# Squares of two groups brought into one step of a state-space scan

## The chip, the cores and the metric

The kernel runs on one core of one Trainium2 chip. The metric is the time of one execution on the device in microseconds (us). A core has engines that run side by side, each with an in-order queue of its own: TensorE (PE in the profile, with PEld for its weight loads), VectorE (DVE), ScalarE (ACT), GpSimd (POOL) and SyncE (SP). An instruction that has to wait holds back all that stand behind it on its engine. Loads are issued from SP's queue and most stores from ACT's; both travel on the same 16 DMA engines. In the profile the DMA queue q1 is the one that SP feeds, and q10 the one that ACT feeds.

## The reference, cut to what matters

One decoder layer: a gated spatial mixer and a Mamba-2 state-space mixer beside each other, merged by gates. The change touches the state-space mixer alone, and in it what comes after the scan:

```python
y_b = ssd_scan(xh, dt, a, bm, cm)                 # 8 groups of 4 heads of 64, chunks of 128 positions
y_b = y_b + xh * d_skip[:, None]
yz = (y_b.reshape(b, s, SSM_D_INNER) * jax.nn.silu(ssm_z)).reshape(b, s, SSM_GROUPS, SSM_D_INNER // SSM_GROUPS)
y_b = rms_norm(yz, ssm_norm_w.reshape(SSM_GROUPS, -1)).reshape(b, s, SSM_D_INNER)
```

The `rms_norm` needs, for each of 8 groups and each of 1024 positions, the sum of the squares of 256 channels. These squares and their sums are what the change moves.

## The kernel before, in words

The program has three long stages: the input projections (up to about 905 us), the state-space stage (to about 1125 us) and the output projections (to the end). All matrix products are split into a high and a low part, so that PE does three products for one.

**The state-space stage.** The scan runs in 32 steps. A step is one group and one pair of chunks (256 positions, called s = 0 to 3). The list `order` (line 1333) takes the groups in pairs: group 0 with s = 0, group 1 with s = 0, group 0 with s = 1, and so on, so even and odd groups alternate. I number the steps by their place n in that list, 0 to 31. In the main loop (lines 1582 to 1592) step n does, in this order: `front` (the products yi within a chunk, and the chunk's state sp), `ahead_of` (work for later steps), `draw` (4 to 6 pairs of matmuls pma of another projection, which fill PE), `back` (the product yn with the incoming state, its evacuation), and `prep` of step n + 2.

**What each engine does for a step.**
- PE: yi, sp, pma, yn, then the products and transposes pc and px for step n + 2.
- ACT: eight exponentials dcy of step n + 2 (line 1167, called decays), two exponentials ea of step n + 3 (line 1155), and the copy bn of step n + 2 (line 1190).
- POOL: a masking select on dcy of step n + 3 (line 1159), which must follow that step's ea; then for the step just done y (1264) and yz (1265); then the products st of the states (1228).
- DVE: the product dcy with pc (1183), xd and xe (1186), the sums into the state st (1236), y (1216) and ym (1262).

Most of them are chained in the order of the program by `link` (line 1111).

**From yz to the norm.** Two steps of a group (s = 0 and 1, or s = 2 and 3) fill one tile yz of two strips of 512 positions. Call that a half, q = 0 or 1. Behind the second of these steps `post` (line 1267) stores both strips to DRAM (`yb_d<-yz`, two DMAs of 256 KB on ACT's queue) and puts down `squares`. `squares` (line 1287) has ACT square both strips in place, so it can start only when the store has read them. Three slots later `sum` (1292) lets POOL add the two strips. Two slots after that `post2` (1296) is put among the `posts`, and the next `front` gives PE four small products pq with 32 output columns each, which sum over the partitions; DVE then writes a row, and ACT stores it (`ms_d`). For q = 1 `post3`, `root` and `post4` follow with a load, a power on POOL (line 1320) and a store. The last pair's q = 1 goes another way (`late_squares`).

**What sets the order.** `later(delay, f)` puts a task down for the slot `slot + delay`, and `run_tasks` counts one slot up and runs what is due. `item` runs it after every front, back and prep, so a step has three slots. `sum` and `root` go to the list `work`, from which `beside_step` takes the first one that is due; `ahead_of` calls it (line 1569). Ranks within an engine are settled by a scheduler at build time; matmuls are pinned in the order of the program.

Of the kernel before, what the change touches and what calls it, by code (L numbers as in the profile page):

```python
# [35 lines left out]
def hybrid_kernel(  # L36
# [56 lines left out]
    def store(dst, src):  # L93
        nc.scalar.dma_start(dst, src)
# [446 lines left out]
    def later(delay, f, *a):  # L541
        tasks.append((slot[0] + delay, f, a))
# [577 lines left out]
    def beside_step():  # L1120

        for w in work:
            if w[0] <= slot[0]:
                work.remove(w)
                w[1](*w[2:])
                return


    class Group:
# [137 lines left out]
        def post(self, q):  # L1267

            g = self.g
            for j in range(2):  # L1270
                store(yb_d[2 * g + j][:, q * 512 : (q + 1) * 512], self.yz[q][:, j])
            yz = self.yz[q]
            if g < NG - 2 or q == 0:
                later(8, self.squares, q, [yz[:, j] for j in range(2)])
            else:
                later(3, self.late_squares)

# [64 lines left out]
    def masks(n):  # L1342
        while done_m[0] < min(n, len(order)):
            g, s = order[done_m[0]]
            groups[g].mask(s)
            done_m[0] += 1

    def decays(n):
        while done_d[0] < min(n, len(order)):
            g, s = order[done_d[0]]  # L1350
            groups[g].decay(s)
            done_d[0] += 1
# [210 lines left out]
    def ahead_of(n):  # L1563

        with tc.high_priority():
            decays(n + 3)
            if n + 1 < len(order) and order[n + 1][1]:
                groups[order[n + 1][0]].mul_state(order[n + 1][1], 0)
            for _ in range(1 if n < 29 else 2):
                beside_step()  # L1570
            masks(n + 4)

# [5 lines left out]
    for n in range(2):  # L1578
        step(n, "front")
        ahead_of(n)  # L1580
        draw(10)
    for n in range(len(order)):
        if n > 1:
            step(n, "front")
            ahead_of(n)
            draw(6 if n == 2 else 4 + n % 2)
        step(n, "back")
        if n == 1:
            draw(4)
        if n + 2 < len(order):  # L1590
            step(n + 2, "prep")
        fetch(n + 6)
    while tasks or work or posts:
# [3 lines left out]
        while posts:  # L1597
            p, q, sq = posts.pop(0)
# [474 lines left out]
```

## Time and profile before

| | us |
|---|---|
| median of 3 runs | 1361.64 (1361.04 to 1362.76) |
| the profiled execution, its own time | 1362.27 |
| its span in the trace | 1360.4 |
| state-space stage, in the trace | about 908 to 1125 |

The profiled execution lies 0.63 us above the median, and 1.9 us of it lie around the span. The granted clock of PE was 0.998 of full speed. Rows of a timeline read: start in us, length in us, engine, line, operation, output<-inputs, shapes, how many instructions (x2), and in brackets how long the engine had been idle and what ended that. ACTq and SPq are DMAs that ACT or SP issue. A run of matmuls is shown a little longer than its place, since its last one drains while the next run starts: the distance of two starts is the cost of a run.

### The profile page before, as it was taken

The numbers are of one execution on the slowest core, as the hardware profiler recorded it, in microseconds if no ns is written. First come the engines' busy times: TensorE is split into PE (matmuls) and PEld (weight loads), VectorE is DVE, ScalarE is ACT, GpSimd is POOL, SyncE is SP. The second block draws the span as 40 slices with busy tenths as digits, with TensorE's granted clock in tenths as the row PEclk, the third lists the DMA queues.
The fourth block names the chain that finished last, engine by engine and source line by source line (L and its number), as shares of the span: only waits on it lengthen the run. The fifth ranks groups of instructions, "written<-read, shape, count | busy, mean of one in ns | idle before, by whom it ended". The sixth has DMA issues, their size and how long they took to land.

```text
span 1360.4 us, 20108 instructions
## 1 busy us (share of the span) xinstructions
PE 1347.0 (99%) x6907; PEld 1114.4 (82%) x6907; DVE 1056.1 (78%) x1731; ACT 800.4 (59%) x1446; POOL 196.1 (14%) x193
## 2 busy tenths in 40 slices
PE   8999999999999999999999999999999999999997
PEld 6688888888888888888888888888888888888886
DVE  4776786787777898688887788358888877959976
ACT  5754666666657665466576655486877834233453
POOL 1000000000000000000000000007798981000002
PEclk9999999999999999999999999999999999999999
DMA  9675444333345667777656866489889878888913
GB/s 292 177 248 142 134 124 124 117 119 122 101 132 155 193 184 231 248 216 246 202 192 193 244 204 186 154 289 318 302 297 311 306 256 291 313 261 317 381 45 124
DMA packets 249577, 288.64 MB, mean 212 GB/s; under 512 B 16860, under 2 KB 196484, under 8 KB 249476
## 3 DMA queue, kind: packets, MB, share of 16 engines
q1 hardware_dynamic: 174868, 203.80, 47.0%
q10 hardware_dynamic: 74544, 83.57, 18.0%
q8 instruction: 54, 0.88, 0.3%
q14 instruction: 47, 0.39, 0.1%
q0 software_dynamic: 64, 0.00, 0.0%
HBM read 199.82 MB, written 87.49 MB: 211 GB/s over the span
## 4 chain that ended last, share of the span: by engine, by line
PE 93%; POOL 3%; DMA 1%; issue 1%; ACT 1%; DVE 1%; SPq 0%; POOLq 0%; DVEq 0%; ACTq 0%
PE xcb L585 6%; PE xz L585 6%; PE xuz L585 6%; PE xx L585 6%; PE xg L585 6%; PE pma L82 5%; PE ox L1914 3%; PE yuz L585 3%; PE yx L585 3%; PE ycb L585 3%; PE yp L1722 3%; PE yz L585 3%; PE vx L990 3%; PE yg L585 3%; PE oy L1914 2%; PE x0p L1722 2%
## 5 line engine op out<-in xcount | busy, mean ns | idle before, releaser
L1159 POOL TENSOR_SCALAR_AFFINE_SELECT dcy<-dcy 128x1024 f32<-128x1024 f32 x32 | 35.3, 1103 | 788.7 <-ACT ea L1155 788.7
L1167 ACT ACTIVATE dcy<-dcy,nacs 128x128 f32<-128x128 f32 x256 | 78.3, 389 | 2.9 <-POOL dcy L1159 2.4
L1183 DVE TENSOR_TENSOR dcy<-dcy,pc 128x1024 f32<-128x1024 f32 x32 | 39.0, 1218 | 8.0 <-PE pc L85 5.8
L1265 POOL TENSOR_TENSOR yz<-y,sl 128x512 f32<-128x512 f32 x32 | 44.7, 1396 | 2.5
L82 PE MATMUL pma<-yh,wah 128*128 128x512 f32 x128 | 43.2, 418 | 0.0
L82 PE MATMUL pma<-yh,wal 128*128 128x512 f32 x128 | 42.6, 413 | 0.0
L82 PE MATMUL pma<-yl,wah 128*128 128x512 f32 x128 | 40.2, 395 | 0.0
L1155 ACT ACTIVATE ea<-dcy 64x512 f32<-64x512 f32 x64 | 39.8, 622 | 0.4
L1190 ACT COPY bn<-pc 128x256 f32<-128x256 f32 x32 | 11.9, 371 | 46.4 <-DVE dcy L1183 44.9
L1060 ACT ACTIVATE ac<-ac 128x1024 f32<-128x1024 f32 x32 | 33.9, 1060 | 8.1 <-DVE ac L1058 7.9
L1264 POOL TENSOR_TENSOR y<-y,ym 128x512 f32<-128x512 f32 (+1 forms) x32 | 37.4, 1170 | 1.8 <-DVE ym L1262 1.8
L1058 DVE SCALAR_TENSOR_TENSOR ac<-c2x,cwt,ac 128x1023 f32<-128x1023 f32 (+2 forms) x24 | 30.7, 1278 | 8.8 <-ACT ac L1056 8.7
L1058 DVE SCALAR_TENSOR_TENSOR ac<-c2cb,cwt,ac 128x1023 f32<-128x1023 f32 (+2 forms) x24 | 30.7, 1278 | 8.2 <-ACT ac L1056 8.0
L1929 POOL TENSOR_TENSOR r<-r,fnw 128x512 f32<-128x512 f32 x4 | 6.1, 1534 | 207.3 <-ACT junk L1927 207.3
L82 PE MATMUL yi<-dcy,xd 128*64 128x128 f32 x512 | 35.0, 279 | 0.0
L1262 DVE TENSOR_TENSOR ym<-yn,ea 128x512 f32<-128x512 f32 (+1 forms) x32 | 19.9, 621 | 18.2 <-PE yn L82 18.0
L1653 DVE SCALAR_TENSOR_TENSOR yn<-yn,par,rb 128x512 f32<-128x512 f32 x32 | 26.1, 822 | 9.1 <-DMA yn<-yb_d 9.1
L82 PE MATMUL sp<-xe,bn 128*128 128x256 f32 x112 | 32.7, 409 | 0.0
L82 PEld LDWEIGHTS yn<-sl,st 128*128 128x128 f32 x224 | 29.8, 191 | 2.8 <-POOL st L1228 0.4
L82 PEld LDWEIGHTS yi<-dcy,xd 128*64 128x64 f32 x512 | 27.3, 136 | 5.7 <-issue 3.2
L1058 DVE SCALAR_TENSOR_TENSOR ac<-c1cb,cwt,ac 128x1023 f32<-128x1023 f32 (+2 forms) x24 | 30.6, 1276 | 1.3 <-ACT ac L1056 1.3
L1022 ACT ACTIVATE vm<-vm,vr 128x128 f32<-128x128 f32 x64 | 25.5, 483 | 10.1 <-DMA vm<-v_d 9.6
(2983 smaller groups left out, 4368.4 us busy)
## 6 DMA issues: line engine op xcount, KB each, us to landing
sl<-s_d SPq DMA_DIRECT2D x32, 768.0 KB
s_d<-ac ACTq DMA_DIRECT2D x32, 512.0 KB
wb_d<-wbb ACTq DMA_DIRECT2D x32, 512.0 KB
dcy<-acs_d SPq DMA_DIRECT2D x32, 512.0 KB
av<-in_w_in_dram SPq DMA_DIRECT2D x36, 256.0 KB
aw<-in_ada_w_dram SPq DMA_DIRECT2D x16, 512.0 KB
wbr<-in_w_proj_b_dram SPq DMA_DIRECT2D x32, 256.0 KB
yb_d<-yz ACTq DMA_DIRECT2D x32, 256.0 KB
```

What stands on the lines that cost most here:

```text
L82: pin(PE.matmul(acc, l, r, start=first, stop=last))
L585: pin(PE.matmul(ps, lw[:, k * P : (k + 1) * P], r[k], start=first and n + k == 0, stop=n == 2 and k == 3, skip_group_check=not first))
L990: pin(PE.matmul(ps[pn][j], l[:, j * P : (j + 1) * P], r, start=nm in ("p1", "p5", "p2") and n + units[i][1] == 0, stop=n == 2 and k == 3, ...
L1058: V.scalar_tensor_tensor(ac[:, s:], cc[:, : S - s], conv_wt[:, 3 - s, i : i + 1], ac[:, s:], op0=ALU.mult, op1=ALU.add)
L1155: link("A", lambda: A.activation(ea[hh * HD : (hh + 1) * HD], dcy.rearrange("p (j e) i l -> p e j (i l)", e=2)[hh * HD : (hh + 1) * HD, hh ...
L1159: link("G", lambda: G.affine_select(out=d8, in_=d8, compare_op=ALU.is_ge, fill=-1e30, base=0, pattern=[[0, 2 * HPG], [1, P]], channel_mult ...
L1167: link("A", lambda: A.activation(dcy[:, h, i, :], dcy[:, h, i, :], AF.Exp, bias=sub[:, i, h : h + 1]))
L1183: link("V", lambda: V.tensor_tensor(d3, d3, pc[:, 0:256].unsqueeze(1).to_broadcast([P, HPG, 256]), op=ALU.mult))
L1264: link("G", lambda: G.tensor_add(y1[:, :, t0:], y1[:, :, t0:], m[:, :, t0:]))
L1265: link("G", lambda: G.tensor_mul(yz, y1, sl[:, 4:6]))
L1722: pin(PE.matmul(ps[j], a[:, v, js], r, start=first and n + k == 0, stop=n == 2 and k == KT - 1, skip_group_check=not first))
L1914: pin(PE.matmul(ps, a[:, tsl], b[:, cs], start=first and n + j == 0, stop=n == 2 and j == 3, skip_group_check=not first))
```

## The change

Two numbers. The odd group's squares are put down for 5 slots instead of 8. The odd group's step is one step, or three slots, behind the even one's, so the squares of both groups fall due in the same slot. And every step may take two items from `work` instead of one, so that both sums can go in one step, and with them both groups' pq in one `front`.

```diff
@@ post
-                later(8, self.squares, q, [yz[:, j] for j in range(2)])
+                later(8 - 3 * (g % 2), self.squares, q, [yz[:, j] for j in range(2)])
@@ ahead_of
-            for _ in range(1 if n < 29 else 2):
+            for _ in range(2):
                 beside_step()
```

No instruction is added or removed. It meets seven halves (both halves of the first three pairs, the first of the last pair). In six of them rows move as in the three places below; in the seventh PE had both pq together already.

**ACT, steps 5 and 6 (first pair, q = 0).** yz_0_8448 is group 0's tile, yz_0_8478 is group 1's, dcy_3_8591 is step 7's decays. The semaphores of the stores of group 1's strips are DMAHW2 and DMAHW5. Before:

```order
L1289 ACTIVATE yz_0_8448<-yz_0_8448 128x512 [waits DMAHW1_49]
L1167 ACTIVATE dcy_3_8591<-dcy_3_8591,nacs 128x128 [waits Pool_49]
...
L1155 ACTIVATE ea_0_8672<-dcy_0_8668 64x512 [waits DMAHW0_49]
L1155 ACTIVATE ea_0_8672<-dcy_0_8668 64x512
L1415 CAST wah_1_8947<-wa_1_8433 128x512 [waits PE_49]
L1528 DMA mt_d_84<-tha_0_8435 128x512 [waits DVE_49]
...
L1190 COPY bn_3_8828<-pc_3_8814 128x256 [waits DVE_49]
L1289 ACTIVATE yz_0_8478<-yz_0_8478 128x512 [waits DMAHW2_49]
L1289 ACTIVATE yz_0_8478<-yz_0_8478 128x512 [waits DMAHW5_49]
```

Now, on ACT in the same place:

```order
L1289 ACTIVATE yz_0_8448<-yz_0_8448 128x512 [waits DMAHW1_49]
L1289 ACTIVATE yz_0_8478<-yz_0_8478 128x512 [waits DMAHW2_49]
L1415 CAST wah_1_8954<-wa_1_8433 128x512 [waits PE_49]
L1528 DMA mt_d_84<-tha_0_8435 128x512 [waits DVE_49]
L1289 ACTIVATE yz_0_8478<-yz_0_8478 128x512 [waits DMAHW5_49]
L1167 ACTIVATE dcy_3_8591<-dcy_3_8591,nacs 128x128 [waits Pool_49]
...
L1155 ACTIVATE ea_0_8672<-dcy_0_8668 64x512 [waits DMAHW0_49]
```

Group 1's two squares, with their waits for that group's store, and the cast wah now stand ahead of step 7's decays and step 8's ea; before they stood behind them.

**POOL, steps 6 and 7.** The sums of the two groups, with the selects of steps 8 and 9. Before:

```order
L1159 AFFINE_SELECT dcy_0_8668<-dcy_0_8668 128x1024
L1264 TENSOR_TENSOR y_2_8761<-y_2_8761,ym_2_8809 128x512
L1265 TENSOR_TENSOR yz_2_8808<-y_2_8761,sl_2_8472 128x2x256
L1228 TENSOR_TENSOR st<-st_8261,cd 128x256
L1293 TENSOR_TENSOR yz_0_8448<-yz_0_8448 128x512
L1159 AFFINE_SELECT dcy_0_8742<-dcy_0_8742 128x1024
```

Now, on POOL in the same place:

```order
L1159 AFFINE_SELECT dcy_0_8668<-dcy_0_8668 128x1024
L1264 TENSOR_TENSOR y_2_8763<-y_2_8763,ym_2_8811 128x512
L1265 TENSOR_TENSOR yz_2_8810<-y_2_8763,sl_2_8472 128x2x256
L1228 TENSOR_TENSOR st<-st_8261,cd 128x256
L1293 TENSOR_TENSOR yz_0_8448<-yz_0_8448 128x512
L1293 TENSOR_TENSOR yz_0_8478<-yz_0_8478 128x512
L1159 AFFINE_SELECT dcy_0_8744<-dcy_0_8744 128x1024
```

Group 1's sum has come forward by one step, right behind group 0's; both still stand behind the select of step 8, which follows step 8's ea.

**PE, front of step 7.** pq are the four products of 32 columns of one group. Before:

```order
L82 MATMUL yi_3_8908<-dcy_3_8591,xd_3_8824 64x128 x8
L82 MATMUL pq_0_8917<-yz_0_8448,ones 32x128 x4
L82 MATMUL sp_3_8924<-xe_3_8826,bn_3_8828 128x256
```

Now, on PE in the same place:

```order
L82 MATMUL yi_3_8909<-dcy_3_8591,xd_3_8826 64x128 x8
L82 MATMUL pq_0_8918<-yz_0_8448,ones 32x128 x4
L82 MATMUL pq_0_8925<-yz_0_8478,ones 32x128 x4
L82 MATMUL sp_3_8932<-xe_3_8828,bn_3_8830 128x256
```

The second pq stood in the front of step 8 before. In the second halves the loads of ssq (SP), the powers (POOL, line 1320) and the stores of ms_d and rs_d (ACT) of the odd group come one step earlier too, next to the even group's.

## The prediction

> **What bounds the kernel now.** I read the page's head first, then the busy time of each engine in the state-space stage (908 to 1125 us), the only stage whose rows move.
>
> ```profile
> span 1360.4 us, 20108 instructions
> core 0: us, PE busy (x) PEld busy (x) DVE busy (x) ACT busy (x) POOL busy (x), PEclk, DMA share, GB/s
> 908.00:1125.00 217.00, 216.85 (x1666) 182.32 (x1665) 178.60 (x309) 151.75 (x393) 173.28 (x165) 1.00 0.88 302
> ```
>
> PE has no gap there: 216.85 of 217 us. So the time changes in two ways only: PE's own work gets shorter, or something makes PE wait. POOL (173.28), DVE (178.60) and the DMA engines (0.88) are close enough behind that a delay of a few us on one of them can reach PE. The timeline of PE shows what the pq cost.
>
> ```profile
> 958.24 1.05 PE L82 MATMUL yn<-sl,st 128*128 128x128 f32 x8
> ...
> 960.33 1.09 PE L82 MATMUL yi<-dcy,xd 128*64 128x128 f32 x16
> 961.35 0.42 PE L82 MATMUL pq<-yz,ones 128*32 128x128 f32 x8
> 961.71 0.70 PE L82 MATMUL sp<-xe,bn 128*128 128x256 f32 x2
> ...
> 1111.75 0.64 PE L82 MATMUL pq<-yz,ones 128*32 128x128 f32 x16
> 1112.33 0.74 PE L82 MATMUL pma<-yl,wah 128*128 128x512 f32 x2
> ```
>
> One group's pq takes 961.71 - 961.35 = 0.36 us of PE. At 1111.75 two groups' pq stand together already and take 1112.33 - 1111.75 = 0.58. Together they save 2 x 0.36 - 0.58 = 0.14 us.
>
> **The gain.** Six pairs come together that did not before: 6 x 0.14 = 0.8 us. That is all that PE's own work can give.
>
> **The cost on ACT.** The timeline of ACT around the first place (first pair, q = 0), and the rows of DMA queue q10, which carries ACT's stores, in three short windows: 952.5 to 953, 953 to 954, and 977 to 978.
>
> ```profile
> 945.87 0.46 ACTq L94 DMA_DIRECT2D yb_d<-yz  x1
> ...
> 950.05 1.15 ACT L1289 ACTIVATE yz<-yz 128x512 f32<-128x512 f32 x2
> 951.11 2.15 ACT L1167 ACTIVATE dcy<-dcy,nacs 128x128 f32<-128x128 f32 x7
> ...
> 953.45 0.61 ACT L1155 ACTIVATE ea<-dcy 64x512 f32<-64x512 f32 x1
> 956.30 1.16 ACT L1289 ACTIVATE yz<-yz 128x512 f32<-128x512 f32 x2
> q10 hardware_dynamic: 24, 0.02, 13.9%
> q10 hardware_dynamic: 2, 0.00, 0.6%
> q10 hardware_dynamic: 11, 0.01, 3.9%
> ```
>
> Group 1's second strip is stored from 945.87. Before, its squares came at 956.30, long after. Now they stand behind group 0's, whose two take 951.11 - 950.05 = 1.06: from 951.11. But q10 still moves 0.02 MB between 952.5 and 953, and nearly nothing in the us after; I take the store as done at 953.5, 7.6 us after its issue. So ACT waits there with the decays of step 7 and the ea of step 8 behind it. The first strip's square and the cast wah fit in the wait. The second square ends 953.5 + 0.53 = 954.0, and the decays start then instead of 951.11: **2.9 us late**, of which 1.06 is the squares' own time.
>
> **From ACT to PE.** The rows of POOL, and two of DVE, in the same place:
>
> ```profile
> 954.77 1.09 POOL L1159 TENSOR_SCALAR_AFFINE_SELECT dcy<-dcy 128x1024 f32<-128x1024 f32 x1 [2.04 <-ACT ea L1155]
> 959.47 1.28 POOL L1293 TENSOR_TENSOR yz<-yz 128x512 f32<-128x512 f32 x1
> 961.02 1.09 POOL L1159 TENSOR_SCALAR_AFFINE_SELECT dcy<-dcy 128x1024 f32<-128x1024 f32 x1 [0.27 <-ACT ea L1155]
> 954.78 1.22 DVE L1183 TENSOR_TENSOR dcy<-dcy,pc 128x1024 f32<-128x1024 f32 x1 [0.25 <-ACT ea L1155]
> 957.71 0.41 DVE L1236 TENSOR_TENSOR st<-st,sp 128x256 f32<-128x256 f32 x1
> ```
>
> The select waits for ea (its bracket says so), so it is late by the same 2.9 and starts at 957.7. From its start to group 0's sum POOL is busy without a gap: 959.47 - 954.77 = 4.7. The sum starts at 962.4, and group 1's now follows 1.25 later (1.28 less the overlap of two rows) and ends at 964.9. PE comes to pq at 961.35 and needs both sums: it is held until 964.9, and sp starts 0.36 later. Against before, sp is 965.3 - 961.71 = 3.55 late; the pq that the next step no longer has gives back 0.36. **Net 3.2 us.** On the way PE may already wait at yn for the state st: DVE is late behind the decays (954.78 needs them), st ended at 958.12, and yn's second half needs it at about 958.24 + 0.44. That wait lies inside the one for pq and is not added.
>
> Same steps for the other half of the first pair and for the first half of the second pair; rows of ACT, POOL and PE of each:
>
> ```profile
> 974.03 1.15 ACT L1289 ACTIVATE yz<-yz 128x512 f32<-128x512 f32 x2
> 975.09 2.44 ACT L1167 ACTIVATE dcy<-dcy,nacs 128x128 f32<-128x128 f32 x8
> 983.01 1.28 POOL L1293 TENSOR_TENSOR yz<-yz 128x512 f32<-128x512 f32 x1
> 985.67 1.13 PE L82 MATMUL sp<-xe,bn 128*128 128x256 f32 x4
> ...
> 995.85 1.13 ACTq L94 DMA_DIRECT2D yb_d<-yz  x2
> 998.87 1.16 ACT L1289 ACTIVATE yz<-yz 128x512 f32<-128x512 f32 x2
> 999.93 2.44 ACT L1167 ACTIVATE dcy<-dcy,nacs 128x128 f32<-128x128 f32 x8
> 1008.30 1.28 POOL L1293 TENSOR_TENSOR yz<-yz 128x512 f32<-128x512 f32 x1
> 1010.54 0.70 PE L82 MATMUL sp<-xe,bn 128*128 128x256 f32 x2
> ```
>
> - Second half: q10 ends in 977 to 978 (0.01 MB), done at 978.0. Decays 978.0 + 0.53 instead of 975.09: 3.4 late. Second sum ends 983.01 + 3.4 + 2.53 = 988.9. Net 988.9 - 985.67 = 3.3.
> - Second pair, q = 0: both stores are issued from 995.85. At 7.6 us as in the first place they end near 1003.4; with the cast and one square after that the decays start near 1004.4, 4.5 late. Second sum ends 1008.30 + 4.5 + 2.53 = 1015.3; net 4.8.
>
> The other three I take at the first two's 3.3. Sum: 3.2 + 3.3 + 4.8 + 3 x 3.3 = 21.2 us, the 0.14 being inside (the first pq runs in the wait). Two bounds. **From below**, every store has landed when its square comes: then ACT is late by 1.06 only (1.6 where the cast moves too). First place: 959.47 + 1.6 + 2.53 - 961.71 = 1.9; second: 983.01 + 1.06 + 2.53 - 985.67 = 0.9; third: 1008.30 + 1.6 + 2.53 - 1010.54 = 1.9. Mean 1.6, sum 9.4 us. **From above**, 21.2 and as much as 5 more, if what is late does not catch up (masks behind two powers of POOL in the second halves, banks asked for earlier by the second pq). I take a value nearer to the upper one, 18: the first place goes by rows of a past that the change does not touch, but each stall of 3 us on PE also lets the loads in flight finish before the next ones are issued, so that later stores should land sooner. I take 0.65 off each of the five places behind it.
>
> The powers, loads and small stores that move in the second halves I cost at nothing: they are the same rows one step earlier, behind the longer waits above. If that cover is gone, two powers in one POOL step cost up to the 1.6 us of the second one, three times; this is in the 5 of the upper bound.
>
> The sum is made against the span of 1360.4; the 1.9 us around it stay. Against the median: 1361.64 + 18 = **1379.6 us**.
>
> **Rivals.**
> 1. *The stores are there in time.* The sum is the lower bound: 1361.6 + 9.4 = 1371. For it: the DMA queues get rest in each stall. Against it: in the first place no stall precedes, and q10's rows run past 952.5. By the Trainium skill (DMA: Bandwidth & Descriptors, Anatomy of one DMA) a DMA takes about 2.0 us plus its bytes at 436 GB/s; as an estimate, 512 KB would land some 3.2 us after the issue, ahead of every square, and the time would be this rival's. The trace speaks against that: q10 carries these strips until 952.5 and longer, over 6 us after the issue, since SP's loads are on the same engines (the DMA share is 0.88).
> 2. *Only the switches are saved.* The place is the front of step 7 and its likes: PE stays unheld if the second sum ends before PE gets to the second pq. Then 1361.6 - 0.8 = 1360.8, within what can't be told from no change (0.2% is 2.7 us); with a stall removed elsewhere it could be slightly faster. It decides from the point where POOL gains 1.3 us or so: group 0's sum ends at 960.75, only 0.6 before PE's 961.35, and the second adds 1.25. For it: POOL idled 2.04 us ahead of the select. Against it: that idle ends with ACT's ea, which gets later.
> 3. *The delays feed on themselves.* POOL's lateness makes the next stores, selects and decays late, and no step catches up: 5 us a place, 30 in all, 1392. For it: POOL and DMA are the busiest beside PE. Against it: the step after a pair has two squares and one sum less on ACT and POOL.
>
> **How the numbers follow.** Main case 0.62 (1373 to 1388), rival 1 0.20 (1367 to 1373), rival 2 0.10, split 0.06 no change and 0.04 faster, rival 3 0.08. The range 1367 to 1389 takes the main case and rival 1. Slower by over 0.2%: 0.62 + 0.20 + 0.08 = 0.90.
>
> **What would show it.** Right: the stage grows from 217 us by about 18; ACT waits at line 1289 for `yb_d<-yz`, 1 to 3 us a place; PE's weight loads for pq wait 2 to 3 us for POOL's line 1293, six times; pq rows read x16. Wrong: no such wait of ACT (rival 1 if pq still wait, rival 2 if not); the time lost elsewhere than at pq and yn; or stalls in the step after a pair (rival 3).

## The result, and the profile after

The change makes the kernel slower: median 1395.22 us (1393.06 to 1397.67, 5 runs) beside 1361.75 (1361.04 to 1362.76, 5 runs) of the kernel before, a ratio of 1.0242 with a 95% interval of 1.0231 to 1.0253. That is 33.5 us more; forecast were 18, in a range up to 27 more. The profiled execution took 1397.67 us, the longest of the five; its account below is of its own span.

The page's head and the busy time of the engines by stretch, of the kernel after (columns: stretch, length, then busy us and instructions of PE, PEld, DVE, ACT, POOL, the granted clock of PE, the DMA share, GB/s):

```profile
span 1396.0 us, 20104 instructions
908.00:940.00 32.00, 32.00 (x213) 26.61 (x212) 29.57 (x47) 22.06 (x55) 13.70 (x14) 1.00 0.99 348
940.00:1125.00 185.00, 166.59 (x1278) 139.18 (x1276) 130.52 (x233) 120.57 (x316) 136.11 (x135) 0.96 0.76 256
1125.00:1160.00 35.00, 30.68 (x193) 24.19 (x192) 26.43 (x43) 13.50 (x29) 23.20 (x20) 0.97 0.67 220
1160.00:1396.00 236.00, 229.12 (x1012) 189.74 (x1011) 184.59 (x306) 89.00 (x167) 11.98 (x11) 0.98 0.68 243
```

Two things are new. Between 940 and 1125 PE stands idle for 185 - 166.59 = 18.4 us, where it had no gap before. And the granted clock, 1.00 there before, is 0.96. What PE waited for is in the view of waits (900 to 1200 us: sum, times, longest), with the one new wait of ACT:

```profile
ACT yz L1289 <- DMA yb_d<-yz: 18.8, 13, 4.3
PE pq L82 <- POOL yz L1293: 7.0, 9, 1.4
PE yn L82 <- DVE st L1236: 6.4, 4, 2.5
PE yn L82 <- DVE xe L1186: 6.1, 3, 4.1
PE x2p L1722 <- DVE tha L1526: 2.9, 1, 2.9
```

PE's four rows add up to 22.4 us. The first three are the chain that was forecast (1.4 of it in the last pair, which was not priced); the fourth lies behind the stage and was not forecast. The first place shows the chain (timeline, rows of ACT, POOL and PE):

```profile
946.93 0.46 ACTq L94 DMA_DIRECT2D yb_d<-yz  x1
951.11 1.15 ACT L1289 ACTIVATE yz<-yz 128x512 f32<-128x512 f32 x2
952.77 0.64 ACT L1289 ACTIVATE yz<-yz 128x512 f32<-128x512 f32 x1 [0.51 <-DMA yb_d<-yz]
954.63 0.63 ACT L1289 ACTIVATE yz<-yz 128x512 f32<-128x512 f32 x1 [0.72 <-DMA yb_d<-yz]
955.17 2.43 ACT L1167 ACTIVATE dcy<-dcy,nacs 128x128 f32<-128x128 f32 x8
958.84 1.09 POOL L1159 TENSOR_SCALAR_AFFINE_SELECT dcy<-dcy 128x1024 f32<-128x1024 f32 x1 [5.01 <-ACT ea L1155]
963.05 2.50 POOL L1293 TENSOR_TENSOR yz<-yz 128x512 f32<-128x512 f32 x2
960.44 0.71 PE L82 MATMUL yn<-sl,st 128*128 128x128 f32 x4 [0.53 <-DVE st L1236]
964.38 0.43 PE L82 MATMUL pq<-yz,ones 128*32 128x128 f32 x8 [0.76 <-POOL yz L1293]
965.61 0.43 PE L82 MATMUL pq<-yz,ones 128*32 128x128 f32 x8 [0.80 <-POOL yz L1293]
```

ACT squares the even group, stands 0.51 us until the odd group's first strip is out, squares it, does the cast, and stands 0.72 us until the second strip is out, 7.7 us after its issue (954.63 - 946.93). The decays start at 955.17. This execution ran 1.05 us later than the one before at this place, so they are 955.17 - 1.05 - 951.11 = 3.0 us late (2.9 forecast). The select and the two sums follow as forecast; PE waits at yn and at both pq.

The clock is seen when stretches are cut at the edges of its record. Four stretches of 3.41 us about the longest wait (4.07 us, until 1020.75), and one about the second place:

```profile
990.76:994.18 3.42, 2.03 (x31) 1.49 (x29) 3.42 (x7) 1.84 (x5) 3.42 (x5) 1.00 0.73 186
1014.66:1018.07 3.41, 2.02 (x9) 1.32 (x7) 1.29 (x2) 3.18 (x11) 0.00 (x0) 1.00 0.58 220
1018.07:1021.48 3.41, 0.73 (x6) 0.76 (x7) 3.30 (x6) 2.57 (x8) 2.10 (x2) 1.00 0.00 0
1021.48:1024.90 3.42, 3.42 (x22) 3.09 (x22) 1.79 (x3) 2.64 (x8) 3.34 (x5) 0.50 0.27 38
1024.90:1028.31 3.41, 3.21 (x36) 2.31 (x35) 3.04 (x8) 0.92 (x3) 3.41 (x3) 1.00 0.88 343
```

In 1018.07 to 1021.48 PE was busy for 0.73 us, and the next stretch runs at 0.50, with PE busy all the time. Behind 2.03 us busy (the first row) and 2.02 (the second) the clock stays at 1.00. Such a stretch costs half of 3.41, 1.7 us. There are four of them between 940 and 1125 and a double one behind 1158, 20.5 us in all. 0.6 us of the double one are still the wait at x2p (until 1158.65), where half clock costs nothing; half of the other 19.9 is lost: **9.9 us at half clock**, beside the waits.

**The account.** 22.5 us of waits (the brackets on PE's timeline); 17 gaps at 0.16 us, since the last matmul ahead of a gap drains past its slot (a pair of pma reads 0.62 and takes 0.46), 2.7; half clock 9.9; 1.1 that this execution was already behind at 880 us: 36.2. Less the 0.8 of the saved switches, which is the forecast's and measured nowhere here, 35.4. The spans differ by 1396.0 - 1360.4 = 35.6.

### The profile page after: what moved, and what is told of

The parts are those of the page before. It is cut to its first block, busy times and chain, and to the rows that moved or that the text cites. A ratio compares the mean times of both kernels' runs of the same rounds, so it can differ in the third digit from the quotient of the medians.

```text
span 1396.0 us, 20104 instructions
## 1 busy us (share of the span) xinstructions
PE 1360.9 (97%) x6907; PEld 1122.9 (80%) x6907; DVE 1057.5 (76%) x1731; ACT 803.8 (58%) x1446; POOL 194.2 (14%) x193
## 4 chain that ended last, share of the span: by engine, by line
PE 82%; POOL 5%; DMA 5%; issue 3%; ACT 3%; DVE 1%; SPq 0%; ACTq 0%; POOLq 0%; DVEq 0%
PE xcb L585 6%; PE xz L585 6%; PE xuz L585 6%; PE xx L585 6%; PE xg L585 5%; PE ox L1914 3%; PE yuz L585 3%; PE yx L585 3%; PE ycb L585 3%; PE vx L990 3%; PE yp L1722 3%; PE yz L585 3%; PE yg L585 3%; PE oy L1914 2%; DMA yb_d<-yz 2%
## 5 line engine op out<-in xcount | busy, mean ns | idle before, releaser
L1167 ACT ACTIVATE dcy<-dcy,nacs 128x128 f32<-128x128 f32 x256 | 78.3, 389 | 17.1 <-POOL dcy L1159 14.8
L82 PE MATMUL yn<-sl,st 128*128 128x128 f32 x224 | 31.9, 280 | 12.6 <-DVE st L1236 6.4
L1060 ACT ACTIVATE ac<-ac 128x1024 f32<-128x1024 f32 x32 | 33.9, 1060 | 8.4 <-DVE ac L1058 8.2
L1262 DVE TENSOR_TENSOR ym<-yn,ea 128x512 f32<-128x512 f32 (+1 forms) x32 | 19.9, 622 | 19.0 <-PE yn L82 18.9
```

Of the source, the lines that this page charges most:

```text
L82: pin(PE.matmul(acc, l, r, start=first, stop=last))
L1167: link("A", lambda: A.activation(dcy[:, h, i, :], dcy[:, h, i, :], AF.Exp, bias=sub[:, i, h : h + 1]))
```

## The experiments

### Landing, bunching, or both

Four kernels part the wait for the store from the meeting of two sums in one step. **Squares only** leaves the second edit out:

```diff
-            for _ in range(2):
+            for _ in range(1 if n < 29 else 2):
```

> Only the first edit: the odd group's squares come three slots nearer, but one queued sum a step as before, so sums and pq of a pair stay in two steps. Theory L (landing: ACT stands at the odd group's squares until its store has landed, and the decays and ea behind them are late): ACT waits at L1289 for yb_d about as long as in the changed kernel (18.8 us between 900 and 1200), PE waits behind it, and most of the 33.5 us stays: 1380 to 1395 us. Theory B (bunching: two sums and two pq in one step hold PE): without the second sum and pq in the step nearly all of it goes: 1361 to 1368. Theory C (each PE wait of some us inside one of the 3.41 us stretches of the clock's record is followed by a stretch at half clock, 1.7 us lost): the time over before is the sum of PE's idle time and 1.7 us per such stretch, whatever the cause of the waits.

**One step only** leaves the first edit out:

```diff
-                later(8 - 3 * (g % 2), self.squares, q, [yz[:, j] for j in range(2)])
+                later(8, self.squares, q, [yz[:, j] for j in range(2)])
```

> Only the second edit: up to two queued sums or powers a step, the squares where they were before. Squares of the two groups come a step apart, so hardly any two sums fall together; only powers and the last pairs move. Theories L and B both: within 2 us of before (1359.5 to 1364). If it is over 5 us slower, the powers that move cost what the prediction had put at nothing.

**Pair late** brings the two groups together at the odd group's old place:

```diff
-                later(8 - 3 * (g % 2), self.squares, q, [yz[:, j] for j in range(2)])
+                later(11 - 3 * (g % 2), self.squares, q, [yz[:, j] for j in range(2)])
```

> Both edits, but the pair comes together at the odd group's old place: delay 11 for the even group and 8 for the odd one. Four squares and two sums stand in one step as in the changed kernel, and both stores have 10 us to land. Theory L: no ACT wait for yb_d at L1289; what is left is the bunching, at most the prediction's lower bound of 9.4 us: 1361 to 1371, no or few stretches at half clock. Theory B: as slow as the changed kernel, 1385 to 1397.

**Squares elsewhere** takes away what the odd group's squares wait for. Room comes from the tiles tha, two instead of four, with their loads moved to k = 4 of a block:

```diff
+            src = sq
+            if self.g % 2:
+                sq = [turn(sq_r, f"sq{self.g}_{q}{j}", F32) for j in range(2)]
             for j in range(2):
-                link("A", lambda: A.activation(sq[j], sq[j], AF.Square))
+                link("A", lambda: A.activation(sq[j], src[j], AF.Square))
```

> The changed kernel, but the odd group's squares are written to two tiles of their own (the four buffers of the gate tiles tha become two, loaded at k = 4 of a block instead of at its start), so they need not wait until the store has read the strip. Squares, sums and pq stand in the same steps as in the changed kernel. Theory L: no ACT wait for yb_d at L1289, 1361 to 1372. Theory B: 1385 to 1397. If the time falls only half the way, both take part.

**Early and apart** is squares elsewhere with the line of squares only.

> Squares three slots nearer and written to tiles of their own (as in the run with the squares elsewhere), but one queued sum a step, so sums and pq stand in two steps as before the change. This is the fourth of four cases: landing wait and bunched sums (the changed kernel: 18.2 us of PE idle between 940 and 1125), landing wait alone (14.7), bunched sums alone (5.6), neither. If the two causes are separate and nearly all of it: 0 to 2 us of PE idle there, 1362 to 1370 us with what the next stage's banks may add (up to 6). If bringing the squares nearer costs by itself (ACT is late by two squares, 1.06 us, at the decays): 4 us or more of PE idle.

The row of the stretch 940 to 1125 of each, in this order: squares only, one step only, pair late, squares elsewhere, early and apart.

```profile
940.00:1125.00 185.00, 170.24 (x1338) 143.47 (x1336) 137.08 (x243) 126.72 (x332) 143.43 (x141) 0.98 0.78 263
```

```profile
940.00:1125.00 185.00, 185.00 (x1467) 156.62 (x1462) 150.75 (x265) 129.94 (x342) 160.55 (x152) 1.00 0.86 293
```

```profile
940.00:1125.00 185.00, 177.09 (x1412) 149.42 (x1406) 146.50 (x255) 126.79 (x335) 152.77 (x147) 1.00 0.82 277
```

```profile
940.00:1125.00 185.00, 179.09 (x1413) 150.73 (x1413) 146.69 (x256) 127.22 (x335) 156.35 (x151) 1.00 0.77 266
```

```profile
940.00:1125.00 185.00, 181.90 (x1425) 153.12 (x1428) 143.17 (x251) 125.37 (x328) 155.16 (x150) 0.99 0.79 270
```

| kernel | squares wait for the store | two sums a step | PE idle, us | ratio to before (95%) |
|---|---|---|---|---|
| the change | yes | yes | 18.4 | 1.0242 (1.0231 to 1.0253) |
| squares only | yes | no | 14.8 | 1.0162 (1.0145 to 1.0178) |
| squares elsewhere | no | yes | 5.9 | 1.0135 (1.0118 to 1.0152) |
| early and apart | no | no | 3.1 | 1.0115 (1.0099 to 1.0130) |
| pair late | no | yes | 7.9 | 1.0111 (1.0093 to 1.0128) |
| one step only | no | hardly | 0.0 | 1.0016 (1.0005 to 1.0026) |

Squares only took 1387.32 us, inside theory L's range, though ACT waits 13.5 us there for the store and not 18.8. One step only took 1366.64 us, 1.7 above the kernel before beside it.

Within the stage the landing theory has most of it: taking the wait away saves 18.4 - 5.9 = 12.5 us with bunched sums and 14.8 - 3.1 = 11.7 without. Bunching takes 3.6 and 2.8. These are single profiles, and a second one of the change (the change again, below) has 22.2 us idle in the same stretch, 3.8 more than the first. So the 12 us of the landing wait stand, but by these sums the price of bunching, and that the two add up as separate causes would, are not shown. That bunching costs something is seen in PE's waits at pq for POOL's sums: 4.8 us with the squares elsewhere, none in early and apart. With neither cause 3.1 us are left, between the two expectations (0 to 2, or 4 and more), 2.2 us of it in one wait at yn; whether that is a price of the nearer squares stays open. ACT's rows in the first place, with the squares elsewhere, show that nothing stands between any more:

```profile
952.67 1.15 ACT L1292 ACTIVATE yz<-yz 128x512 f32<-128x512 f32 x2
953.73 1.14 ACT L1292 ACTIVATE sq<-yz 128x512 f32<-128x512 f32 x2
954.77 0.97 ACT L1167 ACTIVATE dcy<-dcy,nacs 128x128 f32<-128x128 f32 x3
```

But the times miss their expectations: the three kernels without the wait were to be under about 1372 and took 1378 to 1383 us. For two of them, pair late and squares elsewhere, some 3 us of that are not theirs: the kernel before took 1364.94 us beside them (the wait at 924 us below may be the reason). The waits outside the stage tell the rest (PE's waits, 900 to 1200 us, squares elsewhere):

```profile
PE x2p L1727 <- DVE tha L1531: 5.3, 1, 5.3
PE pq L82 <- POOL sq L1296: 4.0, 6, 0.8
PE yn L82 <- POOL st L1228: 2.4, 1, 2.4
PE x0p L1727 <- ACT p1a L1707: 1.1, 1, 1.1
```

Its span is 19.9 us longer than that of before. Of these 5.9 are idle time in the stage, 2.4 a wait at 924 us, ahead of the squares, and 5.3 + 1.1 waits at the next stage's first products. A stretch of 10.2 us at half clock lies there too, but the 5.3 us are inside it, so it costs half of the other 4.9, 2.5 us; 15 drains of 0.16 make 2.4. This kernel also loads the tiles tha later, which may be part of its 5.3. That called for the next two questions.

### The wait at the next stage's first products

The waits written into the built program differ there before anything runs, first before, then after:

```
L1722 MATMUL x2p<-p1bh_10943,p1a_10927 128x512 [waits PE_49]
L1722 MATMUL x2p<-p1bh_10943,p1a_10927 128x512 [waits DVE_49]
```

PSUM banks are given out in turn by a count (line 530). With the pq in other steps the turn shifts, and x2p comes to stand on a bank of the last pma block, which DVE's L1526 frees late. **Banks turned** moves the count on by three at step 29, and **the change again** stands beside it on the same chip:

```diff
             draw(6 if n == 2 else 4 + n % 2)
+            if n == 29:
+                pairs_done.extend([""] * 3)
```

> The changed kernel, with the count that gives out PSUM banks moved on by three at step 29 and nothing else. In the changed kernel the next stage's third product (x2p) stands on the bank that the last block of pma leaves last, and PE waits there 2.9 us for DVE's L1526; in the kernel before no such wait stands in its first products. With the count moved the first products wait for the same things as before. If that wait is an accident of the banks, it goes, and with it the half-clock stretch behind it (6.8 us long, 3.4 lost): 5 to 7 us faster than the changed kernel. If the products are late for another reason (their operands), the wait moves to another row and the time is the same within 2 us.

> The changed kernel once more, beside the next two, because the chip may be another: 1392 to 1402 us. If the account of the first trace holds (22.5 us of PE idle between 940 and 1165, and five places at half clock, 20.5 us long, 10.2 us lost), this trace's idle time and half of its half-clock time add up to its excess over before within 3 us.

The change again took 1395.50 us, 1.0241 (1.0227 to 1.0256) of before; with the banks turned 1390.71, 1.0211 (1.0198 to 1.0225). Where x2p stood still for 2.9 us in the change, it follows at once now; the rows are of the change and then of the kernel with the banks turned:

```profile
1155.39 0.39 PE L1722 MATMUL x1p<-p1bh,p1a 128*128 128x512 f32 x1
1158.65 0.80 PE L1722 MATMUL x2p<-p1bh,p1a 128*128 128x512 f32 x1 [2.88 <-DVE tha L1526]
```

```profile
1154.97 0.39 PE L1724 MATMUL x1p<-p1bh,p1a 128*128 128x512 f32 x1
1155.20 0.39 PE L1724 MATMUL x2p<-p1bh,p1a 128*128 128x512 f32 x1
```

4.8 us are saved, 0.2 short of the expected 5 to 7. The wait (2.87 us in the change again) and one half-clock stretch behind it (1.7) make 4.6. That these two are the 4.8 is not shown: the two profiled spans differ by 6.4 us, 5.5 of it idle time, and both have 17.1 us at half clock, since with the banks turned one more stretch stands inside the stage. What the rows do show is that the wait goes, and that no half clock follows in its place. So the wait belongs to the turn of the banks. The change again agrees with the account: 25.4 us idle and 17.1 us at half clock make 33.9 of the 35.5 by which its span exceeds the first profile of before.

### Does the clock follow PE's waits?

**Gaps filled** puts useless matmuls where PE waits, into the bank that the next matmul overwrites; **half filled** has 7 and 6 in the place of 14 and 12.

```diff
             yn = bank(f"yn{self.g}_{s}")
+            n = order.index((self.g, s))
+            if n > 5 and n % 4 == 2:
+                for _ in range(14):
+                    mm(yn[:, 0:P], ident, ones)
...
+            if g % 2 == 0 and g < NG - 2:
+                for _ in range(12):
+                    mm(pq[:, 0:P], ident, ones)
             for i in range(4):
                 mm(pq[32 * i : 32 * i + 32, 0:P], ones[:, 0:32], sq[0][:, i * P : (i + 1) * P])
```

> The changed kernel with matmuls that are of no use put where PE waits: 14 of 128x128 ahead of yn in each fourth step from step 6 on (places of the waits for st), and 12 ahead of the even group's pq in the six places. They write the bank that the next matmul overwrites. At some 0.11 us each they add 7 x 1.5 + 6 x 1.3 = 18 us of work in the place of about 19 us of waiting. Clock theory (a stretch at half clock follows where PE has stood idle for about half of a 3.41 us stretch): the four half-clock stretches between 940 and 1125 go, each is worth 1.7 us, so the kernel is 3 to 7 us faster than the changed kernel although it does more. If the half clock comes from something else (heat, the load of the chip), the stretches stay and the time is 0 to 6 us above that of the changed kernel.

> As the run with filled gaps, with half as many idle matmuls: 7 ahead of yn, 6 ahead of pq. In that run each took 0.22 us (two rows of 0.11), twice what its expectation assumed, so that they cost 38 us in the place of 22. Now they are 7 x 1.54 + 6 x 1.32 = 18.7 us in the place of some 20 us of waiting. Clock theory: at most one stretch at half clock is left between 940 and 1140 (three or four in the changed kernel), and the kernel is 2 to 6 us faster than the changed one (1390 to 1394). If the clock does not follow PE's idle time: three or four stretches as before, 1395 to 1400.

The stretch 940 to 1125 with the gaps filled, and what 14 of these matmuls took:

```profile
940.00:1125.00 185.00, 184.16 (x1516) 161.77 (x1515) 122.28 (x220) 114.47 (x299) 129.84 (x128) 1.00 0.74 248
957.77 3.29 PE L82 MATMUL yn<-ones,ident 128*128 128x128 f32 x28
960.89 1.06 PE L82 MATMUL yn<-sl,st 128*128 128x128 f32 x8
```

The waits are gone but for 0.8 us, and so is every stretch at half clock in there: 1.00 instead of 0.96. The wait at x2p behind the stage was not filled (3.70 us in this run), and half clock follows it as before. The time was a miss, 1406.76 us (1.0331, 1.0318 to 1.0345): 28 rows for 14 matmuls, 960.89 - 957.77 = 3.12 us, twice my price, so the filling cost more than the waits. With half as many it is 1393.80 us (1.0236, 1.0222 to 1.0250), 1.7 us below the change again in the medians, though PE does some 19 us of useless work. One stretch at half clock is left in the stage, where a wait of 3.22 us outlasted the filling:

```profile
1016.16:1019.57 3.41, 0.29 (x2) 0.33 (x3) 2.86 (x5) 2.57 (x7) 1.66 (x2) 1.00 0.01 3
1019.57:1022.98 3.41, 3.41 (x19) 3.41 (x17) 0.67 (x2) 3.06 (x9) 3.33 (x4) 0.50 0.21 28
```

The intervals of the two overlap, so the time does not decide between the theories; the clock record does. Waits of three different causes (the store's landing, a bank of pma, and in two of five profiles the slow select at 924 us, shown below) were followed by half clock; where those in the stage were filled, it did not come.

### Only what the gain came from

**pq together** takes the kernel before and holds back the even group's pq alone; with **other banks** the count moves on by three at step 29 in place of one at step 31.

```diff
-            later(2, posts.append, (self, q, sq[:1]))
+            later(5 - 3 * (self.g % 2), posts.append, (self, q, sq[:1]))
```

> The kernel before with one thing of the change alone: the even group's pq wait three slots for the odd group's, so that both pq stand in one step; squares and sums stay where they were before, a step apart. (The bank count is moved on by one at step 31, so that the first products of the next stage wait for no pma bank.) This takes the gain of the prediction, 6 x 0.14 = 0.8 us, with none of its costs: 1 us faster to 1 us slower than before. If two pq in one step cost PE in themselves (banks, the second waiting), it is 2 us or more slower.

> As the run with only pq together, but the bank count moved on by three at step 29 in place of one at step 31, so that the last pma blocks stand on banks that the next stage asks for last, as in the run with the banks turned. There, three things cost 9 us that have nothing to do with two pq in a step: 2.4 us at 924 (a select of POOL that took 3.52 us), 3.8 us at a bank of pma, and 1.7 us at half clock. Without the bank's wait: 1361 to 1368; if it is under 1361, this version beats the kernel before. If two pq in one step cost in themselves (1.2 and 1.6 us of waits there), 1364 to 1368.

Slower than before both times: 1371.63 us (1.0064, 1.0052 to 1.0076) and 1367.18 (1.0036, 1.0023 to 1.0049). PE's waits of the second, 900 to 1200 us:

```profile
PE x2p L1724 <- DVE tha L1526: 1.8, 1, 1.8
PE pq L82 <- POOL yz L1293: 1.6, 1, 1.6
PE pq L82 <- DVE xe L1186: 1.2, 1, 1.2
```

They make 4.6 us of the 5.2. The first of the two missed its expectation (within 1 us of before). The bank that I meant to avoid was hit again, and the moved pq wait twice, so two pq in a step cost 2.8 us of waits here. The gain of 0.8 us is smaller than any of these. No version here beats the kernel before.

### The kernel before, once more

> The kernel before, for its profile on this chip: 1361 to 1367 us. If POOL's first select of the stage takes 3.52 us here too (it took 1.09 in the first profile and 3.52 in others), PE waits 2.4 us at 924 in this kernel as well and that wait belongs to no edit.

1361.26 us, no wait of PE and no half clock from 900 to 1350 us, and POOL's first select of the stage took 1.09 us. So the wait at 924 us, seen in 5 of the 14 profiles, was not met in either profile of before. In these five the select took 3.52 us. The rows of POOL and DVE, of before and then of pq together:

```profile
914.74 1.09 POOL L1159 TENSOR_SCALAR_AFFINE_SELECT dcy<-dcy 128x1024 f32<-128x1024 f32 x1 [18.62 <-ACT ea L1155]
914.82 3.36 DVE L1398 TENSOR_TENSOR yl<-yl,yh 128x512 fp32r<-128x512 f32 x4
```

```profile
914.71 3.52 POOL L1159 TENSOR_SCALAR_AFFINE_SELECT dcy<-dcy 128x1024 f32<-128x1024 f32 x1 [18.62 <-ACT ea L1155]
914.78 2.49 DVE L1398 TENSOR_TENSOR yl<-yl,yh 128x512 fp32r<-128x512 f32 x4
```

Both engines start within 0.1 us of each other, and one of them runs slower: DVE's four took 3.36 us beside the quick select and 2.49 beside the slow one. The slow select is longer by 2.43 us, about the 2.49 of the four, as if it stood until they were done. Which comes first seems to be a matter of some ns. All four profiles of one chip have the slow select (squares only, one step only, pair late, squares elsewhere), one of the four of a second and none of the four of a third; and on the first the kernel before took 1364.94 us (13 runs), 2.6 to 3.2 more than on the others. That speaks for the chip or the moment and against an edit, but no profile of before was taken there. It stays open; it is worth 2.4 us, and 1.7 more where half clock follows.

## Why the prediction was right and wrong

**Sign and bottleneck: right; the gain is not shown.** PE bounds the stage, and only a wait could move it far. The saved switches, 0.8 us, show nowhere: in the change the two pq of a pair mostly stand apart with a wait between them.

**The landing wait: right.** ACT waits for `yb_d` 1.2 us at the first place (0.51 + 0.72), then 2.3, 4.6, 1.7, 3.2 and 3.1. With the wait taken away PE's idle time in the stage falls by 12 us or more.

**The sum of the waits: right within 3 us, by a wrong deduction.** PE's waits in the six places are 2.1, 3.6, 4.3, 2.4, 3.1 and 2.7 us, 18.2 in all; with 15 drains of 0.16 they are 20.6, or 19.8 if the 0.8 of the switches was saved: between the 18 forecast and the 21.2 without the deduction. In the first place sp starts at 965.96, less 1.05 for the later run 3.2 us late (3.55 forecast). The 0.65 a place was taken off because stalls should let later stores land sooner. On the whole they don't: from its issue to its square the second strip took 7.7 us at the first place, then 8.4, 7.7, 7.0, 9.0 and 8.1. The chain of waits of the kernel after has

```profile
1007.52 7.64 DMA yb_d<-yz
1062.50 7.96 DMA yb_d<-yz
1092.52 8.05 DMA yb_d<-yz
```

as against the 7.6 us taken in the first place.

**Where PE waits: partly wrong.** "That wait lies inside the one for pq and is not added": it does not add, but it is the larger part. 11.1 of the 18.2 us stand at yn, 7.0 at pq, and pq come as two runs of x8 with a wait between, not as x16. The yn comes first on PE, and st on DVE is late behind the decays.

**Where it failed: in what the sum left out.** The step that failed is the last one, from the waits to the time: it counted a us of wait as one us of time, and it ended with the six places. Missing were half clock (6.8 us in the stage, 3.1 behind it), the wait at x2p for the last pma bank (2.9), and a wait at yn in the last pair (1.4). In that seventh place the squares moved too, and ACT waits 2.6 us for the store; the prediction gave it no price, since both pq stood together there already. These make 14.2 us, beside 19.8 to 20.6 in the six places in place of 18. Two of them could be known before. The trace of before has a stretch at half clock behind a thin one, at its start, which the prediction did not read:

```profile
13.70:17.11 3.41, 1.02 (x5) 0.66 (x6) 3.11 (x7) 3.22 (x6) 0.66 (x2) 1.00 1.02 390
17.11:20.52 3.41, 3.41 (x11) 2.83 (x12) 2.45 (x7) 1.32 (x3) 1.97 (x2) 0.50 1.21 298
```

And the bank's wait stands in the built program, as shown above; the prediction looked at the order of the rows inside the stage, not at the waits behind it.

**The rivals.** Rival 3 came nearest in time (1392) with a mechanism that isn't there: the waits do not grow from place to place, nor stand in the step after a pair. Rival 1's price is near that of the two kernels with two sums a step and the wait for the store gone, within the stage: 5.9 to 7.9 us of PE idle for its 9.4. Its quick landing does not happen: beside the 3.2 us estimated from the Trainium skill (DMA: Bandwidth & Descriptors, Anatomy of one DMA) stand the rows of 7.6 to 8.1. That section gives its figures for DMAs that GpSimd issues; these are ACT's, with SP's loads beside them. Nothing bears out rival 2. **The powers costed at nothing** cost nothing: one step only moves them, and PE has no gap between 940 and 1125.

## What to carry to other kernels

An in-place operation behind a store waits until the store has read its data, here 5 to 9 us after the issue; before moving it nearer, look up the store's landing, and see what is queued behind it on its engine. When an engine without gaps gets gaps of 2 us, price each with the half clock that can follow (1.7 us for a stretch), and when instructions that take a bank in turn move, compare the waits of the next stage's first products as well.

## What was not expected of the hardware

**Half clock after short waits.** I cut the time from 905 to 1180 us of all 14 profiles into the clock record's stretches of 3.41 us. Where PE was idle for 2.0 us or more of a full-clock stretch, the next was at half clock 19 times of 19; with 1.39 to 1.93 us idle, 6 times of 22; with less, never. Several short waits add up: 0.76 + 0.80 us were enough at 963 us. Idle time as a profile shows it is then not quite what decides. The Trainium skill (TensorE: Matmul & The Clock Gate, Part 1 and Why this matters for your kernels) has the free-running window of 3.41 us and the half rate, and the trace agrees with both; it has the rate fall after an idle window and tells to avoid gaps over about 3 us, and there the measurements differ, since 2.0 us were always enough.

**POOL's select against DVE's subtractions**, 1.09 or 3.52 us, as shown above.
